# Both residual additions of a hybrid layer done by accumulating DMAs

## The chip, the cores and the metric

The kernel runs on one core of one Trainium2 chip. The metric is the device time of one execution in microseconds. Three runs of the kernel before gave 1296.79, 1296.92 and 1300.04 us; the median is 1296.92 us. TensorE is called PE, VectorE DVE, ScalarE ACT, GpSimd POOL and SyncE SP.

## The reference

One layer of a streaming encoder, for 1024 prompt tokens and 32 sample tokens (1056 columns, kept with the 1024 model channels as 8 groups of 128 partitions):

```python
xn = rmsnorm(x, pre_mix_norm_w)
proj = xn @ w_in                         # z | xBC | dt | u
# SSD heads on xBC, S5 groups on u -> y_ssd, y_s5
mix = jnp.concatenate([y_ssd, y_s5], axis=-1) @ w_out
h = x + rmsnorm(mix, post_mix_norm_w)                   # first residual addition
up, new_ffn = causal_dwconv(rmsnorm(h, pre_ffn_norm_w) @ w_up, ffn_hist, ffn_conv_w, ffn_conv_b)
gate, val = jnp.split(up, 2, axis=-1)
ffn = (jax.nn.gelu(gate, approximate=True) * val) @ w_down
y = h + rmsnorm(ffn, post_ffn_norm_w)                   # second residual addition
```

The output `y` is the tensor `yT` (128 x 8 x 1056); the states and conv histories are outputs too and are not touched by the change.

## The kernel before

Every float32 matmul is done as three matmuls on split operands (high times high, high times low, low times high): ACT makes the high part of a tile, DVE the low part. Weights come as tiles of 128x1024 (`raw`) that ACT and DVE split into `wh` and `wl` (two buffers each) or, for the down projection, `dh` and `dl`. The tokens are cut into block 0 (one chunk c0 of 512 columns) and block 1 (two chunks c1 and c2 of 272).

The stages, in the order of PE: projections and the S5 and SSD mixers (up to about 385 us); the output projection of block 0 (`gemm_outs(0)`), then its half for block 1 (`gemm_outh2`, whose 16 PSUM tiles ACT copies to `pbo`) with `post(0)` beside it; the FFN of block 0 (`ffn_block(0)`) with the second half for block 1 and `post(1)` inside it; the FFN of block 1 with the finish of block 0 (`fin0`) at its start; and the finish of block 1 (`fin1` for c1, `fin2` for c2), after which the program ends.

`post` (lines 1643 to 1675) makes `h`. For each pair j of channel groups SP loads `x` into a tile `xr` (L1655), DVE scales the branch `o` in place (L1659), POOL adds `xr` (L1660), ACT makes `xh` and DVE `xl` (L1662) for the up projection, and ACT squares `h` into `xr` (or, for the first of each sum, `pacc`), which POOL adds up (L1666) for the next norm; PE sums `pacc` over the partitions. For block 0 SP also stores `h` to the scratch tensor `hd` (L1671).

`fin_out` and `apply` (lines 1860 to 1897) make `y`. ACT has multiplied the FFN sum `acc` by the norm weight; once `sacc` (the norm's factor) is there, one engine multiplies the pair of `acc` by it (L1891) and the same engine adds `h` (L1893 from `o` for block 1, L1896 from `hr`, loaded back from `hd`, for block 0). `fp` names the pairs that POOL does: 1 and 3 of c0 and c1, 3 of c2; the others are DVE's. SP stores each pair (L1897). Three of the four pairs of c1 are held back until DVE has made the last operand of c2's norm (`issue_after`).

The order of instructions on each engine is written by a planner (`Plan`): it lists the operations that touch the same data, gives each a duration and a latency (`cost`), and schedules them forwards and backwards. The engines then run their instructions strictly in the planned order. PE's results of the stages around the change lie in four PSUM buffers (`pch2=(3, 4)`, two buffers each). The program reserves 1024 bytes of every partition as scratch for the descriptors of DMAs that POOL issues (`dynamic_dma_scratch_size=1024`, line 1937); before the change POOL issues none.

Of the kernel before, what the change touches and what calls it, by code (L numbers as in the profile page):

```python
# [9 lines left out]
F32 = mybir.dt.float32  # L10
# [8 lines left out]
KD = D_MODEL // 128  # L19
WA = 512  # L20
# [25 lines left out]
RS_A = RS_C * 2.38924456  # L46
PAR = dict(sp=('x1', 'x2', 'f2'), ia=1, d9=3, pin=1, lat=0.25, uch=1, prep0=6.809, prep1=9.9, prep2=4.066, run0=1.26, run1=6.124, run2=5.94, 
           run3=0.5, uload=6.619, swap_pool=1, z_s5=1, ssd0=13.784, ssd1=0.0, ssd2=2.778, gate0=76.032, glu0=0.384, glu1=2.807, abufs=2, 
           cvat='run7', tcat=1, late_at=2, nsq=1, fg=(), fp=((1, 3), (1, 3), (3,)), fch=(0, (0, 1), 2), pfin=0, q0=0, q1=0, q2=0, nb=0, 
           hv=(), av=(3,), post0=0.802, dn_at=((3, 0), (3, 1)), ob_at=22, sa=2, sb=1, y5b=0, cvb=2.11, msb=(1, 1, 2, 2, 2), pch0=(3,),   # L50
           pch1=(3,), pch2=(3, 4), pf=0, pb=500, pg=0, pn=500, pr=0, pairs=(1, 2, 3, 5, 6), cf=4, cb=1, cg=0, cf2=2, cb2=(0, 1), cg2=0, 
           pgt=500, p5at=1, ng=0, n12=(2, 0), cho=2, dtlag=112.5, ng2=1, pairs2=(1, 2, 3, 5, 6, 7))
# [129 lines left out]
class Plan:  # L182
# [61 lines left out]
    def read(self):  # L244
        ins = [i for i in self.tc.nc.cur_bb.bb.instructions if type(i).__name__ != "BassTilePoolBoundary"]
        n = len(ins)
        self.ins, self.pre = ins, [set() for _ in ins]
        self.eng, self.dur, self.lat = [None] * n, [0.0] * n, [0.0] * n
        self.shared, self.fset, self.bytes = [False] * n, [None] * n, [0] * n
        w, r, use = {}, {}, {}  # L250
        seen, closed = {}, {}

        def aps(l):
            out = []
            for a in l:
                if getattr(a, "bass_ap", None) is not None:
                    k = (a.bass_ap.tensor.name, a.bass_ap.offset, str(a.ap))
                    if k not in seen:
                        seen[k] = self.region(a)
                    out.append((a, seen[k]))  # L260
            return out

        for q, i in enumerate(ins):
            ia, oa = aps(i.ins), aps(i.outs)
            self.cost(q, i, ia, oa)
            for _, g in ia:
                self.pre[q].update(k for k, h in w.get(g[0], ()) if self.meet(g, h))
            for _, g in oa:
                for d in (w, r):
                    self.pre[q].update(k for k, h in d.get(g[0], ()) if self.meet(g, h))  # L270
            for _, g in oa:
                for d in (w, r):
                    d[g[0]] = [(k, h) for k, h in d.get(g[0], ()) if not self.holds(g, h)]
                w[g[0]].append((q, g))
                use.setdefault(g[0], []).append(q)
            for _, g in ia:
                r.setdefault(g[0], []).append((q, g))
                use.setdefault(g[0], []).append(q)
            if type(i).__name__ == "InstMatmult":
# [62 lines left out]
    def cost(self, q, i, ia, oa):  # L342
        self.eng[q] = e = str(i.engine).split(".")[-1]
        kind = type(i).__name__
        n = max(self.free(a) for a, _ in ia + oa)
        if kind == "InstDMACopy":
            self.bytes[q] = 4 * int(np.prod([m for _, m in ia[0][0].ap]))
            self.dur[q], self.lat[q] = 0.06, 2.0
            return
        if kind == "InstMatmult":  # L350
            n, m = (self.free(a) for a, _ in ia[:2])
            if ia[0][0].dtype == F32R:
                d = max(0.43 * n + 6, 107 if m > 64 else 54)
            elif i.is_transpose:
                d = 112
            else:
                d = 2 * max(0.85 * n, 108) if m > 64 else 0.85 * n
            self.dur[q], self.lat[q] = d * 1e-3, 0.07
            return
        big = [a for a, _ in ia if self.free(a) > 1]  # L360
        ps = any(g[0].startswith(("ms", "pm")) for _, g in ia)
        if kind == "InstActivation":
            self.fset[q] = str(i.func).split(".")[-1]
            d = 0.19 + 0.00085 * n + 0.08 * (len(ia) > len(big))
        elif e == "Pool":
            self.shared[q] = len(big) > 1
            d = 0.21 + 0.00165 * n if len(big) > 1 else 0.12 + 0.0009 * n
        else:
            self.shared[q] = not ps and n > 8
            d = 0.15 + (0.00105 if ps or len(big) > 1 else 0.00053) * n  # L370
        self.dur[q] = d

    def schedule(self, rank, pre, suc, forward=True, gate=None):
# [12 lines left out]
        while todo:  # L386
# [26 lines left out]
            start[q] = s = t  # L413
            order[e].append(q)
            if self.bytes[q]:
                if forward:
                    s = max(s, lanes[0])
                free[e] = s + self.dur[q]
                wire = max(wire, s + 0.9) + self.bytes[q] / 280e3
                end[q] = max(s + self.lat[q], wire + 0.8)  # L420
                lanes = lanes[1:] + [end[q]]
            else:
                if self.shared[q]:
                    s = max(s, lock)
# [34 lines left out]
def body(tc, xT, wt, wdt, vec, cst, dtp, hist4, hist3, h0ssd, s5p, s5bc, s5d, glu, glub,  # L459
# [286 lines left out]
    y_dram = [dram.tile([128, 4, NCH5], F32, name=f"yd{i}") for i in range(8)]  # L746
    z_dram = dram.tile([128, 4, T], F32, name="zd")
    pb_dram = dram.tile([128, KD, T - WA], F32, name="pbd")
    h_dram = dram.tile([128, KD, WA], F32, name="hd")

    ext4 = {}

# [890 lines left out]
    def post(b):  # L1643
        HN[b] = xtiles(b)
        for c in BLKC[b]:
# [6 lines left out]
            yield 2  # L1652
            for j in range(4):
                xr = iot("xr")[:, :, :w]
                D.dma_start(xr, xT[:, 2 * j:2 * j + 2, t0:t0 + w])  # L1655
                for kk in range(2):
                    k = 2 * j + kk
                    h = O[b][:, k, o:o + w]
                    V.scalar_tensor_tensor(h, h, vc("post_mix", k), r1, mult, mult)  # L1659
                    (V if k in par["hv"] else G).tensor_tensor(h, h, xr[:, kk], add)  # L1660
                    act(xh[:, k, :], h, AF.Copy, scale=vc("pre_ffn", k))
                    V.scalar_tensor_tensor(xl[:, k, :], h, vc("pre_ffn", k), xh[:, k, :].bitcast(F32), mult, sub)  # L1662
                    e = V if k in par["av"] else G
# [196 lines left out]
    def fin_out(c):  # L1860
# [13 lines left out]
        if c == 1:
            ap = [(1, j) for j in par["fp"][1]] + [(1, j) for j in range(4) if j not in par["fp"][1]][:par["ia"]]
        elif c == 2:
            ap = [(1, j) for j in range(4) if j not in par["fp"][1]][par["ia"]:] + ap
        with ExitStack() as es:
            if c == 2:
                es.enter_context(tc.issue_after(last[0].ins))  # L1880
            for c_, j in ap:
                apply(c_, j)
                yield 0.9

    def apply(c, j):
        t0, w = CHUNKS[c]
        b = int(c > 0)
        o = t0 - BLK[b][0]
        a = ACC[b][:, 2 * j:2 * j + 2, o:o + w]
        e = G if j in par["fp"][c] else V  # L1890
        e.tensor_tensor(a, a, fin[c][0][:, None, :].to_broadcast([128, 2, w]), mult)  # L1891
        if b:
            e.tensor_tensor(a, a, O[b][:, 2 * j:2 * j + 2, o:o + w], add)  # L1893
        else:
            for kk in range(2):
                e.tensor_tensor(a[:, kk], a[:, kk], hrs[2 * j + kk], add)  # L1896
        D.dma_start(yT[:, 2 * j:2 * j + 2, t0:t0 + w], a)  # L1897

    hrs = {}

    def fin_block(b):
        if b == 0:
            for j, n in enumerate(("ext0", "ext1", "W0", "G0", "T0", "C0")):
                h = tl(n, [128, 2 if j < 2 else 1, 512], "hr")
                k = 2 * j if j < 2 else j + 2
                D.dma_start(h, h_dram[:, k:k + h.shape[1]])
                for i in range(h.shape[1]):
                    hrs[k + i] = h[:, i]
# [37 lines left out]
```

## Time and profile before

| What | us |
|---|---|
| median of three runs | 1296.92 |
| the profiled execution | 1294.34 |
| its span (first to last instruction) | 1292.4 |
| PE busy | 1225.8 (95%) |
| DVE busy | 1035.2 (80%) |
| ACT busy | 574.5 (44%) |
| POOL busy | 397.7 (31%) |
| PE granted clock, mean | 0.979 |

PE is busy for 95% of the span, so the time can only change by what PE waits for, and by what lies behind PE's last matmul. The remaining 66.6 us in which PE is not busy are read stretch by stretch. A row of a timeline gives start, duration, engine, line, operation and operands; a count `x4` behind it means that four instructions are merged, and the bracket names the idle time before them and what ended it.

### The profile page before, as it was taken

The page shows a single profiled execution, that of the slowest core. Times are in us where ns is not written, and L with a number is a line of the kernel's source. Part 1 is how long each engine was busy: PE and PEld are TensorE (multiplying, and loading weights), DVE is VectorE, ACT ScalarE, POOL GpSimd, SP SyncE. Part 2 cuts the span into 40 slices and gives each one's busy share as a digit, 9 for nine tenths or more (in the row PEclk, how much of TensorE's full clock was granted, in tenths as well). Part 3 has the DMA queues.
Part 4 walks back from the last instruction along what each step waited for, and adds up shares of the span by engine and source line. Part 5 has one row for each costly group of instructions (what it writes and reads, how often), then busy time and mean ns, then how long its engine had stood idle before and what let it go on. Part 6 is the DMA issues. An engine that isn't in the chain of part 4 may idle for free.

```text
span 1292.4 us, 20981 instructions
## 1 busy us (share of the span) xinstructions
PE 1225.8 (95%) x7880; PEld 1105.6 (86%) x7880; DVE 1035.2 (80%) x1781; ACT 574.5 (44%) x979; POOL 397.7 (31%) x577
## 2 busy tenths in 40 slices
PE   6879999999998999999999999998999999999995
PEld 5768888888877888878977888887999999999994
DVE  7898887988988998987688977679577777777777
ACT  7236466554555555543444433353523333333243
POOL 5364554544146433211345110015111111111113
PEclk8989999999998999999999999999999999999997
DMA  7133323233434423234433333222323332222212
GB/s 220 57 96 99 96 76 114 79 106 93 124 105 164 152 91 99 81 104 137 153 99 123 122 99 98 95 85 82 117 81 98 99 98 82 95 86 83 82 52 70
DMA packets 66901, 132.14 MB, mean 102 GB/s; under 512 B 13936, under 2 KB 34800, under 8 KB 66800
## 3 DMA queue, kind: packets, MB, share of 16 engines
q1 hardware_dynamic: 66800, 130.81, 32.2%
q8 instruction: 62, 1.02, 0.3%
q14 instruction: 39, 0.32, 0.1%
HBM read 111.69 MB, written 15.81 MB: 99 GB/s over the span
## 4 chain that ended last, share of the span: by engine, by line
PE 79%; DVE 10%; POOL 3%; issue 3%; DMA 2%; ACT 1%; SPq 1%; DVEq 0%; ACTq 0%; POOLq 0%
PE pm L479 70%; PE ms L479 9%; DVE wl L713 1%; POOL pacc L1666 1%; POOL o L1660 1%; DVE o L1659 1%; SPq L1122 1%; DMA xst<-xT 1%; DVE scr L647 1%; DVE scr L646 1%; POOL oacc L1628 1%; PE ms L483 1%; DVE pq L996 1%; POOL hq L1164 0%; DVE yr L1104 0%
## 5 line engine op out<-in xcount | busy, mean ns | idle before, releaser
L479 PE MATMUL pm<-xh,wh 128*128 128x272 f32 (+1 forms) x1616 | 532.1, 330 | 15.9 <-ACT wh L535 8.7
L479 PE MATMUL pm<-xh,wl 128*128 128x272 f32 (+1 forms) x1616 | 531.1, 329 | 7.4 <-DVE wl L713 7.3
L479 PE MATMUL pm<-xl,wh 128*128 128x272 f32 (+1 forms) x1616 | 529.8, 328 | 1.7 <-DVE xl L1045 1.7
L479 PEld LDWEIGHTS pm<-xh,wh 128*128 128x128 f32 x1616 | 309.9, 192 | 37.8 <-ACT wh L535 8.7
L479 PEld LDWEIGHTS pm<-xh,wl 128*128 128x128 f32 x1616 | 309.0, 191 | 30.8 <-DVE wl L713 9.1
L479 PEld LDWEIGHTS pm<-xl,wh 128*128 128x128 f32 x1616 | 309.9, 192 | 24.4 <-DVE xl L1045 3.0
L535 ACT ACTIVATE wh<-raw 128x1024 fp32r<-128x1024 f32 x120 | 126.9, 1057 | 177.5 <-PE pm L479 109.5
L713 DVE TENSOR_TENSOR wl<-raw,wh 128x1024 fp32r<-128x1024 f32 x120 | 154.9, 1291 | 26.6 <-ACT wh L535 26.1
L479 PE MATMUL pm<-al,dh 128*128 128x272 f32 (+1 forms) x528 | 171.4, 325 | 0.6 <-DVE al L1751 0.6
L479 PE MATMUL pm<-ah,dh 128*128 128x272 f32 (+1 forms) x528 | 171.7, 325 | 0.3 <-ACT ah L535 0.3
L479 PE MATMUL pm<-ah,dl 128*128 128x272 f32 (+1 forms) x528 | 170.8, 324 | 0.0
L1793 DVE TENSOR_TENSOR acc<-acc,pm 128x272 f32<-128x272 f32 (+1 forms) x235 | 121.1, 520 | 53.6 <-PE pm L479 52.5
L1738 DVE SCALAR_TENSOR_TENSOR ftmp<-fext,vec_t,ftmp 128x512 f32<-128x512 f32 (+1 forms) x176 | 143.1, 814 | 3.9 <-ACT ftmp L535 2.1
L1716 POOL COPY fext<-halo 128x2 f32<-128x2 f32 x88 | 33.6, 382 | 293.0 <-DVE ftmp L1738 271.5
L1721 DVE TENSOR_TENSOR fext<-pm,rbc 128x512 f32<-128x512 f32 (+2 forms) x132 | 67.5, 511 | 69.2 <-PE pm L479 65.8
L479 PEld LDWEIGHTS pm<-ah,dh 128*128 128x128 f32 x528 | 99.4, 188 | 8.6 <-ACT ah L535 0.7
L479 PEld LDWEIGHTS pm<-al,dh 128*128 128x128 f32 x528 | 99.3, 188 | 8.1 <-DVE al L1751 0.9
L479 PEld LDWEIGHTS pm<-ah,dl 128*128 128x128 f32 x528 | 99.2, 188 | 7.7 <-issue 0.3
L535 ACT ACTIVATE dh<-raw 128x1024 fp32r<-128x1024 f32 (+1 forms) x46 | 46.7, 1018 | 108.3 <-PE pm L479 96.8
L535 ACT ACTIVATE ftmp<-fext,vec_t 128x512 f32<-128x512 f32 (+1 forms) x88 | 72.3, 822 | 11.1 <-DVE fext L1721 5.7
L535 ACT ACTIVATE ftmp<-ftmp 128x512 f32<-128x512 f32 (+1 forms) x44 | 28.4, 644 | 87.0 <-DVE ftmp L1738 87.0
L1771 DVE TENSOR_TENSOR dl<-raw,dh 128x1024 fp32r<-128x1024 f32 (+1 forms) x46 | 55.9, 1216 | 13.6 <-ACT dh L535 13.6
(318 smaller groups left out, 1668.7 us busy)
## 6 DMA issues: line engine op xcount, KB each, us to landing
raw<-wt SPq DMA_DIRECT2D x164, 512.0 KB, 3.3
gluw<-glu SPq DMA_DIRECT2D x8, 512.0 KB, 3.4
xst<-xT SPq DMA_DIRECT2D x16, 136.0 KB, 3.3
pbd<-pbo SPq DMA_DIRECT2D x8, 272.0 KB, 2.6
xr<-xT SPq DMA_DIRECT2D x8, 272.0 KB, 3.2
pbi<-pbd SPq DMA_DIRECT2D x8, 272.0 KB, 3.5
yT<-acc SPq DMA_DIRECT2D x8, 272.0 KB, 2.3
ud<-uext SPq DMA_DIRECT2D x4, 528.0 KB, 4.0
```

The costliest lines, as they stand in the source:

```text
L479: PE.matmul(out, lhsT, rhs, start=start, stop=stop, **kw)
L483: PE.transpose(out, in_, ident)
L535: S.activation(out, in_, func, bias=bias, scale=scale)
L646: e.tensor_scalar(hi[:L, o:o + L], ident[:L, :L], r[:L, i:i + 1], None, mult)
L647: last[0] = V.scalar_tensor_tensor(lo[:L, o:o + L], ident[:L, :L], r[:L, i:i + 1], hi[:L, o:o + L].bitcast(F32), mult, sub)
L713: V.tensor_tensor(lo, r, hi.bitcast(F32), sub)
L996: V.tensor_scalar(pq[lo:hi, a], src[lo:hi, :, o:o + 8], sg, None, mult)
L1716: G.tensor_copy(e[:, 0:2], halo[:, j, :])
L1721: V.tensor_tensor(e[:, 2 + o:2 + o + wp], ps[:, :wp], rbc[:, t0:t0 + wp], mult)
L1738: V.scalar_tensor_tensor(t, e[:, i:i + n], vc("fw", 3 * j + i), t, mult, add)
L1771: V.tensor_tensor(l, rr, h.bitcast(F32), sub)
L1793: V.tensor_tensor(a, a, ps[:, :w], add)
```

## The change

The scaled branch stays in `o`, and a DMA that POOL issues adds `x` to it in SBUF (`accum_op=add`): the eight scalings of a chunk go in pairs, and for each pair one DMA of 128x2x512 or 128x2x272 reads `xT` and accumulates into `o`. Nothing else reads `xT` there; `xr` is only the place for squares. The finished `h` of every chunk is stored to `yT` by SP. In the finish DVE does all the multiplications by the norm factor, and a second DMA of POOL accumulates the product onto `yT`. The additions on POOL and DVE, the scratch tensor `hd` with its loads, and the holding back of c1's pairs are gone; `fp` is empty. The planner gets a cost for POOL's DMAs (1.0 us of POOL, 3.5 us of latency), slightly other matmul costs, and an order between reads of one PSUM tile by the same engine. Since the planner works on the whole program, it writes a new order for all of it; the counts of all other instructions stay, but ACT has 21 loads of its function tables in place of 18.

```diff
-           cvat='run7', tcat=1, late_at=2, nsq=1, fg=(), fp=((1, 3), (1, 3), (3,)), fch=(0, (0, 1), 2), pfin=0, ...
+           cvat='run7', tcat=1, late_at=2, nsq=1, fg=(), fp=((), (), ()), fch=(0, (0, 1), 2), pfin=0, ...
...
             for _, g in ia:
+                if g[0].startswith(("ms", "pm")):
+                    self.pre[q].update(k for k, h in r.get(g[0], ()) if self.eng[k] == self.eng[q])
...
-            self.dur[q], self.lat[q] = 0.06, 2.0
+            self.dur[q], self.lat[q] = (0.06, 2.0) if e == "SP" else (1.0, 3.5)
...
-                d = max(0.43 * n + 6, 107 if m > 64 else 54)
+                d = max(0.426 * n + 9, 107 if m > 64 else 54)
...
-                D.dma_start(xr, xT[:, 2 * j:2 * j + 2, t0:t0 + w])
+                for kk in range(2):
+                    h = O[b][:, 2 * j + kk, o:o + w]
+                    V.scalar_tensor_tensor(h, h, vc("post_mix", 2 * j + kk), r1, mult, mult)
+                G.dma_start(O[b][:, 2 * j:2 * j + 2, o:o + w], xT[:, 2 * j:2 * j + 2, t0:t0 + w], accum_op=add)
                 for kk in range(2):
                     k = 2 * j + kk
                     h = O[b][:, k, o:o + w]
-                    V.scalar_tensor_tensor(h, h, vc("post_mix", k), r1, mult, mult)
-                    (V if k in par["hv"] else G).tensor_tensor(h, h, xr[:, kk], add)
...
-                if b == 0:
-                    D.dma_start(h_dram[:, 2 * j:2 * j + 2], O[b][:, 2 * j:2 * j + 2, o:o + w])
+                D.dma_start(yT[:, 2 * j:2 * j + 2, t0:t0 + w], O[b][:, 2 * j:2 * j + 2, o:o + w])
...
-        e = G if j in par["fp"][c] else V
-        e.tensor_tensor(a, a, fin[c][0][:, None, :].to_broadcast([128, 2, w]), mult)
-        if b:
-            e.tensor_tensor(a, a, O[b][:, 2 * j:2 * j + 2, o:o + w], add)
-        else:
-            for kk in range(2):
-                e.tensor_tensor(a[:, kk], a[:, kk], hrs[2 * j + kk], add)
-        D.dma_start(yT[:, 2 * j:2 * j + 2, t0:t0 + w], a)
+        V.tensor_tensor(a, a, fin[c][0][:, None, :].to_broadcast([128, 2, w]), mult)
+        G.dma_start(yT[:, 2 * j:2 * j + 2, t0:t0 + w], a, accum_op=add)
```

On ACT in `post(0)`, the kernel before takes each `h` soon after it is there, with copies of PE's results (`pbo`) in between:

```order
L535 ACTIVATE pbo<-pm 128x272 x2
L535 ACTIVATE pacc<-o_3883 128x512
L535 ACTIVATE xh_4057<-o_3883,vec_t 128x512
L535 ACTIVATE pbo<-pm 128x272
L535 ACTIVATE xr<-o_3883 128x512
L535 ACTIVATE xh_4057<-o_3883,vec_t 128x512
L535 ACTIVATE xr<-o_3883 128x512
L535 ACTIVATE pbo<-pm 128x272 x2
L535 ACTIVATE wh<-raw 128x1024
```

The same place of the changed kernel; the eight reads of `o` as `pacc` and `xr` are those of the four DMAs in turn, two each:

```order
L538 ACTIVATE pacc<-o_3882 128x512
L538 ACTIVATE xr<-o_3882 128x512
L538 ACTIVATE pbo<-pm 128x272 x2
L538 ACTIVATE xh_4056<-o_3882,vec_t 128x512 x2
L538 ACTIVATE xr<-o_3882 128x512
L538 ACTIVATE pacc<-o_3882 128x512
L538 ACTIVATE xr<-o_3882 128x512 x2
L538 ACTIVATE wh<-raw 128x1024
L538 ACTIVATE xr<-o_3882 128x512 x2
L538 ACTIVATE pbo<-pm 128x272 x2
```

In the changed kernel the squares of the second, third and fourth DMA, with one `wh`, stand between two groups of `pbo`.

On DVE in `post(0)`, before, the scalings (L1659) stand ahead of two splits of weights:

```order
L647 SCALAR_TENSOR_TENSOR scr<-cst_t,nry,scr 128x128
L1659 SCALAR_TENSOR_TENSOR o_3883<-o_3883,vec_t,oacc 128x512 x7
L713 TENSOR_TENSOR wl<-raw,wh 128x1024
L1659 SCALAR_TENSOR_TENSOR o_3883<-o_3883,vec_t,oacc 128x512
L713 TENSOR_TENSOR wl<-raw,wh 128x1024
```

and in the changed kernel (L716 is the split):

```order
L650 SCALAR_TENSOR_TENSOR scr<-cst_t,nry,scr 128x128
L716 TENSOR_TENSOR wl<-raw,wh 128x1024
L1659 SCALAR_TENSOR_TENSOR o_3882<-o_3882,vec_t,oacc 128x512 x8
L716 TENSOR_TENSOR wl<-raw,wh 128x1024
L1665 SCALAR_TENSOR_TENSOR xl_4057<-o_3882,vec_t,xh_4056 128x512 x2
```

One split has moved ahead of the scalings.

On POOL at the end of the program, before, after the four sums of squares (`sacc`):

```order
L1857 TENSOR_TENSOR sacc<-sacc,osq 128x272 x4
L1891 TENSOR_TENSOR acc_8887<-acc_8887,sacc 128x2x272
L1893 TENSOR_TENSOR acc_8887<-acc_8887,o_6230 128x2x272
L1891 TENSOR_TENSOR acc_8887<-acc_8887,sacc 128x2x272
L1893 TENSOR_TENSOR acc_8887<-acc_8887,o_6230 128x2x272
L1891 TENSOR_TENSOR acc_8887<-acc_8887,sacc 128x2x272
L1893 TENSOR_TENSOR acc_8887<-acc_8887,o_6230 128x2x272
```

and in the changed kernel:

```order
L1735 COPY o_4431<-fext 128x2
L1736 COPY o_4431<-fext 128x2
L1859 TENSOR_TENSOR sacc<-sacc,osq 128x272 x4
L1886 DMA yT<-acc_8850 128x2x272 x8
L1920 UNCONDITIONAL_BRANCH
```

Six tensor operations of POOL have become eight DMA issues, four of c1 and four of c2, and they are POOL's last work; on DVE the eight multiplications stand as four ahead of c2's norm and four behind it.

## Rows read from the trace of the kernel before

**Rows 1.** The page's first part: busy time, share, instructions.
```profile
span 1292.4 us, 20981 instructions
PE 1225.8 (95%) x7880; PEld 1105.6 (86%) x7880; DVE 1035.2 (80%) x1781; ACT 574.5 (44%) x979; POOL 397.7 (31%) x577
```
**Rows 2.** Busy time by stretch: PE, PEld, DVE, ACT, POOL, PE clock, DMA share, GB/s.
```profile
0.00:385.00 385.00, 349.30 (x2245) 309.93 (x2246) 327.76 (x576) 202.45 (x420) 177.39 (x208) 0.97 0.36 106
385.00:440.00 55.00, 48.97 (x322) 45.10 (x321) 46.77 (x62) 27.22 (x48) 36.59 (x21) 0.94 0.46 154
640.00:715.00 75.00, 71.43 (x369) 58.27 (x368) 62.12 (x130) 33.15 (x63) 38.12 (x43) 1.00 0.39 121
870.00:925.00 55.00, 49.55 (x361) 47.96 (x361) 44.95 (x69) 23.88 (x38) 25.13 (x30) 0.94 0.31 106
1255.00:1292.40 37.40, 21.51 (x168) 20.35 (x166) 27.46 (x61) 14.24 (x34) 12.79 (x10) 0.76 0.18 60
```
**Rows 3.** PE's longest waits at 385 to 445 and 875 to 925: total, times, longest.
```profile
PE pm L479 <- DVE wl L713: 4.2, 1, 4.2
...
PE pm L479 <- DVE fext L1721: 4.1, 1, 4.1
```
**Rows 4.** Timeline in post(0): start, us, engine, line, operation, idle before.
```profile
399.70 0.40 ACT L535 ACTIVATE pbo<-pm 128x272 f32<-128x272 f32 x1 [1.11 <-PE pm L479]
401.77 9.92 DVE L1659 SCALAR_TENSOR_TENSOR o<-o,vec_t,oacc 128x512 f32<-128x512 f32 x7 [1.22 <-ACT oacc L535]
411.61 2.28 DVE L713 TENSOR_TENSOR wl<-raw,wh 128x1024 fp32r<-128x1024 f32 x1
420.62 3.97 POOL L1660 TENSOR_TENSOR o<-o,xr 128x512 f32<-128x512 f32 x2
```
**Rows 5.** DMA issues with KB each and us to landing; one stretch of SP.
```profile
xr<-xT SPq DMA_DIRECT2D x8, 272.0 KB, 3.2
xr<-xT SPq DMA_DIRECT2D x4, 512.0 KB, 3.6
yT<-acc SPq DMA_DIRECT2D x8, 272.0 KB, 2.3
xst<-xT SPq DMA_DIRECT2D x8, 256.0 KB, 5.1
...
2.12 6.30 SPq L1041 DMA_DIRECT2D xst<-xT  x11
```
**Rows 6.** Timeline of post(1): scalings and last sums of both chunks; PE's first wait.
```profile
655.28 2.77 DVE L1659 SCALAR_TENSOR_TENSOR o<-o,vec_t,oacc 128x272 f32<-128x272 f32 x4
666.36 4.10 POOL L1666 TENSOR_TENSOR pacc<-pacc,xr 128x272 f32<-128x272 f32 x3
670.52 1.23 PE L479 MATMUL ms<-onec,pacc 128*128 128x1 f32 x12 [0.98 <-POOL pacc L1666]
682.74 2.76 DVE L1659 SCALAR_TENSOR_TENSOR o<-o,vec_t,oacc 128x272 f32<-128x272 f32 x4
698.89 2.59 POOL L1666 TENSOR_TENSOR pacc<-pacc,xr 128x272 f32<-128x272 f32 x2
```
**Rows 7.** Timeline of DVE in fin0.
```profile
889.36 1.22 DVE L1891 TENSOR_TENSOR acc<-acc,sacc 128x1024 f32<-128x1024 f32 x1
890.62 4.49 DVE L1896 TENSOR_TENSOR acc<-acc,hr 128x512 f32<-128x512 f32 x2
```
**Rows 8.** Timeline of the finish of block 1.
```profile
1273.55 1.58 DVE L1891 TENSOR_TENSOR acc<-acc,sacc 128x544 f32<-128x544 f32 x1
1276.35 13.36 SPq L1897 DMA_DIRECT2D yT<-acc  x8
1282.46 0.40 ACT L535 ACTIVATE sacc<-ms 128x272 f32<-128x272 f32 x1 [7.76 <-PE ms L479]
1287.84 0.72 DVE L1891 TENSOR_TENSOR acc<-acc,sacc 128x544 f32<-128x544 f32 x1
```
**Rows 9.** The group of ACT's table loads: busy, mean ns.
```profile
L535 ACT ACT_TABLE_LOAD x18 | 23.1, 1283 | 10.6 <-DVE yr L900 6.1 <-DMA xst<-xT 4.2
```

More of the change, by code (lines that the diff above doesn't have):

```diff
@@ L48 @@
            run3=0.5, uload=6.619, swap_pool=1, z_s5=1, ssd0=13.784, ssd1=0.0, ssd2=2.778, gate0=76.032, glu0=0.384, glu1=2.807, abufs=2,
-           cvat='run7', tcat=1, late_at=2, nsq=1, fg=(), fp=((1, 3), (1, 3), (3,)), fch=(0, (0, 1), 2), pfin=0, q0=0, q1=0, q2=0, nb=0,
+           cvat='run7', tcat=1, late_at=2, nsq=1, fg=(), fp=((), (), ()), fch=(0, (0, 1), 2), pfin=0, q0=0, q1=0, q2=0, nb=0,
            hv=(), av=(3,), post0=0.802, dn_at=((3, 0), (3, 1)), ob_at=22, sa=2, sb=1, y5b=0, cvb=2.11, msb=(1, 1, 2, 2, 2), pch0=(3,),
@@ L415, in schedule @@
             if self.bytes[q]:
-                if forward:
+                if forward and e == "SP":
                     s = max(s, lanes[0])
@@ L419, in schedule @@
                 wire = max(wire, s + 0.9) + self.bytes[q] / 280e3
-                end[q] = max(s + self.lat[q], wire + 0.8)
-                lanes = lanes[1:] + [end[q]]
+                end[q] = max(s + self.dur[q] + self.lat[q], wire + 0.8)
+                if e == "SP":
+                    lanes = lanes[1:] + [end[q]]
             else:
@@ L748, in body @@
     pb_dram = dram.tile([128, KD, T - WA], F32, name="pbd")
-    h_dram = dram.tile([128, KD, WA], F32, name="hd")
     ext4 = {}
@@ L1873, in fin_out @@
         ap = [(c, j) for j in range(4)]
[L1874 to L1883, printed above, removed]
+        for c_, j in ap:
+            apply(c_, j)
+            yield 0.9
     def apply(c, j):
@@ L1889, in apply @@
         a = ACC[b][:, 2 * j:2 * j + 2, o:o + w]
-        e = G if j in par["fp"][c] else V
-        e.tensor_tensor(a, a, fin[c][0][:, None, :].to_broadcast([128, 2, w]), mult)
-        if b:
-            e.tensor_tensor(a, a, O[b][:, 2 * j:2 * j + 2, o:o + w], add)
-        else:
-            for kk in range(2):
-                e.tensor_tensor(a[:, kk], a[:, kk], hrs[2 * j + kk], add)
-        D.dma_start(yT[:, 2 * j:2 * j + 2, t0:t0 + w], a)
-    hrs = {}
-    def fin_block(b):
[L1902 to L1908, printed above, removed]
+        V.tensor_tensor(a, a, fin[c][0][:, None, :].to_broadcast([128, 2, w]), mult)
+        G.dma_start(yT[:, 2 * j:2 * j + 2, t0:t0 + w], a, accum_op=add)
+    def fin_block(b):
         for c in BLKC[b]:
```

## The prediction

> **What bounds the kernel now.** I read the page's first part, then the busy time by stretch, then in each stretch with idle time what PE waited for, and last the timelines there. PE is busy for 1225.8 of 1292.4 us [rows 1], so 66.6 us are all that a change can win from PE's waits and the tail. Five stretches hold them: 35.7 up to 385 us, 6.0 around `post(0)`, 3.6 around `post(1)`, 5.5 around `fin0` and 15.9 in the last 37.4 (length less PE's busy time) [rows 2]. The change acts in the last four. In `post(0)` the largest wait of PE is 4.2 us for a `wl`, in `fin0` 4.1 us for a `fext` [rows 3]. The `wl` starts at 411.61 and stands directly behind seven scalings that took 9.92 [rows 4]. DVE's row in `fin0` shows the like: 1.22 and 4.49 us of finish work in one piece [rows 7]. In `post(1)` PE waits 0.98 for the last sum of squares [rows 6]. At the end PE has nothing left: the order is factor, products, additions and stores, and the last store's issue ends at 1289.71 (1276.35 + 13.36) [rows 8], 2.7 before the span's end.
>
> **The open price: how fast POOL can issue accumulating DMAs.** No row shows POOL issuing any DMA, nor any accumulating one; all terms of the sum but one hang on the time from one such DMA to the next, which I call p. SP's loads of the same 272 KB land 3.2 us after issue, 512 KB 3.6; a store of 272 KB lands after 2.3 [rows 5]. SP hands over eleven loads in 6.30, 0.57 each, while each takes 5.1 to land [rows 5]: SP waits for no landing. For POOL I assume that it does: the program leaves 1024 bytes of a partition for descriptors, and each of these DMAs names 256 rows as source and, to add, the same rows of the destination as a second source. So p is an issue and a landing: 0.57 + 3.2 = 3.8 us, for 512 KB 4.2, by the rows that are nearest. Bounds: 2.3, if the landing is that of a store and the issue lies inside it; 6.9, if the issue takes as long as a sum on POOL (4.10 / 3 = 1.37 [rows 6]) and destination's read and write follow each other (1.37 + 3.2 + 2.3); for 512 KB 7.3.
>
> No row shows such a limit. [...]
>
> **The tail, +12.7.** Before, DVE could take the first product of c1 at 1273.55 [rows 8]. Its rows of 128x544 take 0.72 where POOL does not work beside (1.58 where it does) [rows 8]; in the changed kernel POOL makes no sums there, so the first DMA can be issued at 1274.27. POOL has eight, four of c1, four of c2. At one per 3.8 the last lands at 1274.27 + 30.4 = 1304.7; c2's products cannot be late, since its factor is there at 1282.86 (1282.46 + 0.40) [rows 8], and POOL's fifth DMA starts at 1289.5. Of the 2.7 behind the last issue before, 2.3 were landing [rows 5], so 0.4 stay: 1305.1, against 1292.4. What went, additions of 0.72 to 1.87, was itself shorter than a DMA. Bounds: p = 2.3 gives 1293.1 (+0.7), p = 6.9 gives 1329.9 (+37.5).
>
> **`post(0)`, +2.4.** The `wl` has moved ahead of the scalings, and these no longer have POOL's sums beside them (9.92 / 7 = 1.42 each; 0.72 by the row of a similar size [rows 4, 8]): the wait of 4.2 goes. What is late next is ACT, which copies PE's results out (`pbo`). From 401.77 the first pair is scaled at 403.2; its DMA lands at 407.4 and two squares (0.40 each by ACT's row [rows 4]) end at 408.2. Then come two `pbo`, and the next stand behind the squares of the other three DMAs, which land 4.2 apart: 408.2 + 12.6 = 420.8. PE has four buffers, each 1.5 us of its work (0.40 + 1.11, ACT's rhythm there [rows 4]), so 6.0 of 12.6 are covered and 6.6 are a new wait. Net +2.4. The chain itself is no later: the last DMA lands at 403.2 + 16.8 = 420.0, and before, POOL's last sum ended at 424.59 [rows 4]. Bounds: with all of it hidden -4.2; with 7.3 for a DMA 21.9 - 6.0 - 4.2 = +11.7. SP's store of `h` replaces that to `hd`, at nothing: SP is not what anything waits for.
>
> **`post(1)`, +6.0.** Four scalings take 2.77 and 2.76 [rows 6], so the first pair of c1 is there at 656.7, of c2 at 684.1. Four DMAs later (15.2) two squares (0.8) and two sums (2.59 [rows 6]) follow: 675.3 and 702.7. Before, the sums ended at 670.46 and 701.48 [rows 6], the first already 0.98 too late for PE. So +4.8 and +1.2, the second on top since all behind the first shifts. ACT's splits and gelu and POOL's `halo` copies queue behind the same DMAs; I cost them at nothing, as the FFN's next tiles cover them, and they become a cost if that cover goes. Bounds: -1.0 (the wait goes) and, at p = 6.9, 17.2 + 13.6 = +30.8.
>
> **`fin0`, -4.1.** DVE has four products of 1.22 and none of the additions (4.49 for two [rows 7]); POOL issues between its small copies. The wait for `fext` goes. Bounds: -4.1 and 0, if `fext`'s copies on POOL stand behind DMAs for as long.
>
> **The rest, 0.** Up to 385 us the work is re-planned with three more table loads of 1.283 us [rows 9], 3.8 us if all were on PE's path; the waits there (35.7) can move by as much the other way: 0, bounds of 4 to either side.
>
> Sum: 12.7 + 2.4 + 6.0 - 4.1 = +17.0. The profiled execution took 1294.34 (span and 1.94), so 1311.3. It lay 2.6 under the median of 1296.92, so I forecast 1313.9. Each us of p is worth 19 (8 in the tail, 3, and 4 twice).
>
> **Rivals.** *POOL hands over as SP does*, 0.57 apart. For it: that SP's rows show it, and that nothing in the trace shows a limit for POOL. Then the `wl` wait goes (-4.2), `post(1)` loses its 0.98, `fin0` 4.1, and at the end c2's factor at 1282.86 is followed by four products of 0.72, one issue, one landing of 3.2 and the 0.4: 1289.9, -2.5. Together -11.8: 1285.1, faster. It decides as soon as two DMAs are in flight at once.
>
> *One at a time, but short*: p = 2.9 (0.57 and a store's 2.3). Tail 1274.27 + 23.2 + 0.4, +5.5; `post(0)` 9.9 (3.3 each) - 10.2 = -0.3; `post(1)` +1.2; `fin0` -4.1; sum +2.3, 1299.2. Against it: loads of these sizes needed 3.2 and 3.6. [...]
>
> *Long*: the accumulate reads, then writes, and POOL's issue is as slow as its sums. From p = 5.0 on: 1313.9 + 1.2 x 19 = 1337, up to 1381 with all upper bounds.
>
> *The new order decides*: waits up to 385 us change by 4, with p as in the second rival, 1295 to 1303.
>
> **How the numbers follow.** A measurement of this kernel can tell 0.3%, 3.9 us, from no change: 1293.0 to 1300.8. Chances: the forecast 0.55 (p from 3.0 to 5.0, 1299 to 1337), POOL back to back 0.18, short 0.14, long 0.08, the order 0.05. Faster is the first rival and the lowest part of the short one, 0.22; the same, most of the short one and part of the order, 0.11; slower 0.67. The range goes from the first rival's 1285 to 1338, and leaves out the long case and what lies below.
>
> **What would show it.** In the tail: eight issues of L1886 some 3.8 us apart, each at the landing of the one before, the chain of waits ending in POOL's last DMA, and DVE idle. Issues 1 us apart or less prove the first rival. In `post(0)`: ACT waiting for `o` from a DMA, PE for `pbo`; in `post(1)` PE waiting 5 us or more for `pacc`. The waits of 4.2 for `wl` and 4.1 for `fext` should be gone; if either stands, that term is wrong. If the last issue of POOL lies before 1287, the sum is wrong as a whole.

## The result and the profile after

The changed kernel takes 1349.74 us (median of 4 runs, 1346.77 to 1351.18) against 1298.48 of the kernel before, run beside it: a ratio of 1.039, interval 1.0361 to 1.0419. It is slower, as forecast, but by three times as much: the forecast was +17.0 us, its range ended at 1338, and the profiled execution is 56.8 us longer by span (1349.2 against 1292.4).

The page's first part of the changed kernel, in the columns of [rows 1]:

```profile
span 1349.2 us, 20951 instructions
PE 1234.8 (92%) x7880; PEld 1113.5 (83%) x7880; DVE 1008.1 (75%) x1777; ACT 575.4 (43%) x982; POOL 364.1 (27%) x565
```

DVE and POOL have less to do than before (27.1 and 33.6 us less) and the kernel is longer: their busy time is not what counts. PE is now idle for 114.4 us (66.6 before), which is 47.8 of the 56.8 us; the other 9.0 are longer busy time of the same 7880 matmuls, at a mean granted clock of 0.955 (0.979 before). By stretch, in the columns of [rows 2]:

```profile
0.00:385.00 385.00, 348.75 (x2216) 308.77 (x2217) 329.28 (x571) 200.41 (x418) 169.00 (x204) 0.96 0.35 101
385.00:440.00 55.00, 35.65 (x242) 33.01 (x240) 27.27 (x41) 18.39 (x34) 25.77 (x17) 0.86 0.57 143
640.00:715.00 75.00, 66.90 (x390) 58.65 (x390) 48.16 (x116) 30.91 (x58) 23.81 (x31) 0.93 0.45 122
```

In the first stretch PE is idle for as long as it was (36.3 us, 35.7 before), but does 29 matmuls fewer there; `post(0)` has 19.4 us of idle PE where it had 6.0, and the granted clock of that stretch fell from 0.94 to 0.86. The third holds the first half of `post(1)`'s waits (8.1 idle, 3.6 before). PE's longest waits (total, times, longest), where before there was 4.2 for `wl` and 4.1 for `fext` [rows 3]:

```profile
PE pm L482 <- ACT pbo L538: 19.1, 1, 19.1
PE ms L482 <- POOL pacc L1669: 17.2, 2, 9.1
...
PE pm L482 <- ACT acc L538: 2.2, 2, 2.0
...
PE pm L482 <- DVE wl L716: 1.2, 1, 1.2
```

The waits that were to go are gone (`wl` 1.2 in all, `fext` 0.3), and two others add up to 36.3 us: `pbo`, which is new, and `pacc`, which was 2.3 before. The timeline of `post(0)` in the changed kernel shows DVE's scalings, POOL's issues and what ACT waits for (start, duration, engine, line; the bracket is the idle time before it and what ended it):

```profile
406.77 5.39 DVE L1659 SCALAR_TENSOR_TENSOR o<-o,vec_t,oacc 128x512 f32<-128x512 f32 x8
```

```profile
408.51 1.41 POOL L1660 DMA_DIRECT2D o<-xT  x1 [7.87 <-DVE o L1659]
415.80 1.23 POOL L1660 DMA_DIRECT2D o<-xT  x1 [5.88 <-issue]
425.11 1.21 POOL L1660 DMA_DIRECT2D o<-xT  x1 [8.07 <-issue]
432.06 1.22 POOL L1660 DMA_DIRECT2D o<-xT  x1 [5.74 <-issue]
```

```profile
416.68 0.67 ACT L538 ACTIVATE pbo<-pm 128x272 f32<-128x272 f32 x2
417.23 1.33 ACT L538 ACTIVATE xh<-o,vec_t 128x512 fp32r<-128x512 f32 x2
424.93 0.63 ACT L538 ACTIVATE xr<-o 128x512 f32<-128x512 f32 x1 [6.36 <-DMA o<-xT]
425.46 0.61 ACT L538 ACTIVATE pacc<-o 128x512 f32<-128x512 f32 x1
431.82 1.15 ACT L538 ACTIVATE xr<-o 128x512 f32<-128x512 f32 x2 [5.74 <-DMA o<-xT]
432.87 1.04 ACT L538 ACTIVATE wh<-raw 128x1024 fp32r<-128x1024 f32 x1
438.84 1.15 ACT L538 ACTIVATE xr<-o 128x512 f32<-128x512 f32 x2 [4.93 <-DMA o<-xT]
439.90 0.66 ACT L538 ACTIVATE pbo<-pm 128x272 f32<-128x272 f32 x2
```

DVE had scaled all eight groups by 412.2 (406.77 + 5.39), yet POOL issues its fourth DMA at 432.06: the DMAs come 7.3, 9.3 and 7.0 us apart, each "issue" of the bracket being a wait for nothing that the profile shows. ACT has no `pbo` between 417.3 and 439.9, so PE's four buffers stay full and PE waits 19.1 us. The tail has the same picture; the first product and six of the eight issues are

```profile
1307.33 0.72 DVE L1885 TENSOR_TENSOR acc<-acc,sacc 128x544 f32<-128x544 f32 x1
```

```profile
1308.46 1.21 POOL L1886 DMA_DIRECT2D yT<-acc  x1 [3.31 <-DVE sacc L1859]
1313.31 1.22 POOL L1886 DMA_DIRECT2D yT<-acc  x1 [3.63 <-DVE nry L629]
1318.15 1.21 POOL L1886 DMA_DIRECT2D yT<-acc  x1 [3.62 <-DVE acc L1885]
...
1333.00 1.22 POOL L1886 DMA_DIRECT2D yT<-acc  x1 [3.81 <-issue]
1338.01 1.21 POOL L1886 DMA_DIRECT2D yT<-acc  x1 [3.79 <-issue]
1342.94 1.22 POOL L1886 DMA_DIRECT2D yT<-acc  x1 [3.72 <-issue]
```

They are 4.8 to 5.0 us apart, 4.93 on average, while DVE has finished the last product at 1318.1. (The first waits for its product. The releasers named in the next two brackets only happen to end just before: c1's four products were there at 1310.3, and neither `nry` nor c2's products are read by these DMAs. The even spacing suggests that from the second on all wait for the same thing.) The DMA table has the landing times, counted from the start of the issue, to be set beside [rows 5]:

```profile
o<-xT POOLq DMA_DIRECT2D x8, 272.0 KB, 4.7
yT<-o SPq DMA_DIRECT2D x8, 272.0 KB, 2.4
yT<-acc POOLq DMA_DIRECT2D x8, 272.0 KB, 4.6
...
o<-xT POOLq DMA_DIRECT2D x4, 512.0 KB, 6.9
yT<-o SPq DMA_DIRECT2D x4, 512.0 KB, 3.0
yT<-acc POOLq DMA_DIRECT2D x4, 512.0 KB, 6.0
```

In the tail the next issue starts 0.3 us after the landing of the one before. So the mechanism of the forecast stands (one accumulating DMA at a time) and its price does not: 4.93 in place of 3.8, and 7.0 to 9.3 in place of 4.2.

### The profile page after: what moved, and what is told of

Same layout as the page of the kernel before. It is cut to its first block, busy times and chain, and to the rows that moved or that the text cites. A ratio compares the mean times of both kernels' runs of the same rounds, so it can differ in the third digit from the quotient of the medians.

```text
span 1349.2 us, 20951 instructions
## 1 busy us (share of the span) xinstructions
PE 1234.8 (92%) x7880; PEld 1113.5 (83%) x7880; DVE 1008.1 (75%) x1777; ACT 575.4 (43%) x982; POOL 364.1 (27%) x565
## 4 chain that ended last, share of the span: by engine, by line
PE 72%; DVE 10%; issue 7%; DMA 4%; ACT 3%; POOL 2%; SPq 1%; POOLq 0%; ACTq 0%; DVEq 0%
PE pm L482 62%; PE ms L482 9%; DMA o<-xT 2%; SPq L1124 1%; DVE wl L716 1%; DMA raw<-wt 1%; ACT wh L538 1%; POOL yT L1886 1%; DVE R L1164 1%; PE ms L486 1%; DVE xl L1047 0%; DVE scr L649 0%; DMA yT<-acc 0%; DVE ftmp L1740 0%; ACT xh L538 0%
## 5 line engine op out<-in xcount | busy, mean ns | idle before, releaser
L482 PE MATMUL pm<-xh,wh 128*128 128x272 f32 (+1 forms) x1616 | 532.5, 330 | 28.8 <-ACT pbo L538 19.1
L482 PEld LDWEIGHTS pm<-xh,wh 128*128 128x128 f32 x1616 | 310.5, 192 | 51.5 <-ACT pbo L538 19.3
L716 DVE TENSOR_TENSOR wl<-raw,wh 128x1024 fp32r<-128x1024 f32 x120 | 156.1, 1301 | 48.4 <-ACT wh L538 48.2
L1740 DVE SCALAR_TENSOR_TENSOR ftmp<-fext,vec_t,ftmp 128x512 f32<-128x512 f32 (+1 forms) x176 | 138.4, 787 | 13.9 <-ACT ftmp L538 11.6
```

What stands on the lines that cost most here:

```text
L482: PE.matmul(out, lhsT, rhs, start=start, stop=stop, **kw)
L716: V.tensor_tensor(lo, r, hi.bitcast(F32), sub)
L1740: V.scalar_tensor_tensor(t, e[:, i:i + n], vc("fw", 3 * j + i), t, mult, add)
```

## The experiments

Theory A: POOL's descriptor room holds one accumulating DMA of 256 rows, so each waits for the landing of the one before. Rival B: POOL waits for a landing whatever the room. Beside it stands the question how much of the loss is the new order of the whole program. The edits of the first four runs, against the changed kernel (e1) or as the part of the change that is kept (e2 to e4, main lines only):

```diff
 e1
-    nc = bacc.Bacc("TRN2", target_bir_lowering=False, num_devices=1, dynamic_dma_scratch_size=1024)
+    nc = bacc.Bacc("TRN2", target_bir_lowering=False, num_devices=1, dynamic_dma_scratch_size=1536)
 e2: the kernel before with
+                if g[0].startswith(("ms", "pm")):
+                    self.pre[q].update(k for k, h in r.get(g[0], ()) if self.eng[k] == self.eng[q])
...
-                d = max(0.43 * n + 6, 107 if m > 64 else 54)
+                d = max(0.426 * n + 9, 107 if m > 64 else 54)
...
-                end[q] = max(s + self.lat[q], wire + 0.8)
+                end[q] = max(s + self.dur[q] + self.lat[q], wire + 0.8)
...
 e3: e2 with
...
+                G.dma_start(O[b][:, 2 * j:2 * j + 2, o:o + w], xT[:, 2 * j:2 * j + 2, t0:t0 + w], accum_op=add)
...
 e4: e2 with
...
+        G.dma_start(yT[:, 2 * j:2 * j + 2, t0:t0 + w], a, accum_op=add)
...
```

The third edit of e2 belongs to the planner's cost of DMAs: it also lets SP's DMAs end up to 0.06 us later in the plan.

**e1, more room.** 

> The changed kernel with 1536 instead of 1024 bytes of descriptor room, nothing else (the planned order is the same). Theory A (room for one accumulating DMA only, so POOL's next one waits for the landing, 4.96 us apart in the tail): two fit, the spacing in the tail falls to about 2.5 us, the tail shortens by some 17 us, the waits of PE for pbo (19.1) and pacc (17.2) fall by about half, in all about 1300 to 1315 us. Rival B (POOL waits for a landing whatever the room): spacing stays at 4.9 and the time at 1345 to 1352 us.

Measured: 1305.18 us, 1.0066 (1.004 to 1.0092) of before. The order of the instructions is that of the changed kernel; 512 bytes take 44.6 us away. POOL in the tail:

```profile
1284.10 2.46 POOL L1886 DMA_DIRECT2D yT<-acc  x2 [3.31 <-DVE sacc L1859]
1288.97 1.21 POOL L1886 DMA_DIRECT2D yT<-acc  x1 [2.41 <-DVE nry L629]
1291.28 1.20 POOL L1886 DMA_DIRECT2D yT<-acc  x1 [1.09 <-issue]
1293.92 1.22 POOL L1886 DMA_DIRECT2D yT<-acc  x1 [1.44 <-DVE acc L1885]
```

Two issues stand back to back, the third follows 4.9 us after the first, when that has landed: two in flight, 2.4 us apart on average. PE's wait for `pbo` is 10.2 and for `pacc` 4.8. Theory A as expected, B is out.

**e2, the plan alone.** 

> The kernel before with only the planner's changed costs and the order between reads of a PSUM tile; no accumulating DMA. Theory A (the first scaling of post(0) came 5.0 us later in the changed kernel because the new order is worse up to there): 1300 to 1304 us. Rival (the new order is neutral and the 5 us come from something that the DMAs bring): 1294 to 1299 us.

Measured: 1306.64 us, 1.0067 (1.0047 to 1.0087): a loss of 9.9 without any DMA of POOL, above the range of 1300 to 1304 that I expected. Its first scaling starts at 412.9 (401.8 before), and ACT has 26 loads of its function tables (18 before).

**e3, the first addition alone.** 

> Planner as changed, the first addition by accumulating DMAs, the finish as in the kernel before. Theory A: the PE waits for pbo and pacc stand (some 30 us more than before), the tail is as before, 1325 to 1338 us. Rival (the loss sits in the finish and in the tail alone): under 1310 us.

Measured: 1334.9 us, 1.0286 (1.0248 to 1.0324), 28.3 over e2. PE's two waits are there as in the changed kernel, 18.6 for `pbo` and 18.3 for `pacc`, and `fext`'s of 4.0 stays, as DVE keeps its additions in `fin0`.

**e4, the second addition alone.** 

> Planner as changed, post as in the kernel before (with h stored to yT), the second addition by accumulating DMAs. Theory A: the tail costs some 23 us, fin0's wait for fext goes (-4), 1313 to 1325 us. Rival (the tail is late only because the stages ahead delay it): 1295 to 1303 us.

Measured: 1325.96 us, 1.0222 (1.0188 to 1.0257), just over the expected range; 19.3 over e2. Its eight DMAs in the tail start at 1284.45 to 1318.95, 4.93 apart. The parts add up: 1306.6 + 28.3 + 19.3 = 1354.2, against 1349.7 for both.

**e5, DMAs of half the rows, 1024 bytes.** In the changed kernel, each DMA is cut by channel group:

```diff
-                G.dma_start(O[b][:, 2 * j:2 * j + 2, o:o + w], xT[:, 2 * j:2 * j + 2, t0:t0 + w], accum_op=add)
+                    G.dma_start(h, xT[:, 2 * j + kk, t0:t0 + w], accum_op=add)
...
-        G.dma_start(yT[:, 2 * j:2 * j + 2, t0:t0 + w], a, accum_op=add)
+        for kk in range(2):
+            G.dma_start(yT[:, 2 * j + kk, t0:t0 + w], a[:, kk], accum_op=add)
```

> The changed kernel with 1024 bytes of room as it is, each accumulating DMA of 256 rows cut into two of 128 rows (24 + 24 in place of 12 + 12). Theory A (POOL waits because the room is full; the run with 1536 bytes took 2 DMAs of 256 rows, so 1024 bytes should take three or so of 128 rows): first three issues back to back at 1.2 us, then pairs of halves some 2.5 to 3.5 us apart in place of 4.96, 1308 to 1325 us. Rival B (one DMA at a time, whatever its size; more room only helped in another way): each half about 4 us, a pair 8 us, the tail 20 us longer than in the changed kernel, over 1370 us.

Measured: 1320.11 us, 1.0181 (1.0131 to 1.0231): twice as many DMAs and 29.6 us less than the changed kernel. POOL in the tail:

```profile
1295.10 2.70 POOL L1887 DMA_DIRECT2D yT<-acc  x3
1298.67 0.86 POOL L1887 DMA_DIRECT2D yT<-acc  x1 [0.87 <-issue]
```

Three go out without a gap, and the fourth starts 3.57 us after the first, whose kind lands after 3.5. So it is the room that counts. A half has half the bytes too, but in `post(0)` of this run the halves have 256 KB each, nearly the 272 KB of which only one is in flight in the changed kernel, and again three go out:

```profile
414.98 2.88 POOL L1660 DMA_DIRECT2D o<-xT  x3 [7.09 <-DVE o L1659]
421.16 0.89 POOL L1660 DMA_DIRECT2D o<-xT  x1 [3.30 <-issue]
```

So the room is used by rows and not by bytes: three halves are in flight here, one DMA of 256 rows in the changed kernel, two in e1. My estimate from these counts, if nothing but the room holds POOL and equal DMAs take equal shares of it: one of 256 rows takes over 512 and at most 768 of the bytes reserved in a partition, one of 128 rows over 256 and at most 341.

**e6, the plan told the truth, 1024 bytes.**

```diff
-            self.dur[q], self.lat[q] = (0.06, 2.0) if e == "SP" else (1.0, 3.5)
+            self.dur[q], self.lat[q] = (0.06, 2.0) if e == "SP" else (5.0, 0.1)
```

> The changed kernel with 1024 bytes of room, but the planner is told what the trace of the changed kernel showed: POOL is taken for 5.0 us by an accumulating DMA and the data is there 0.1 us later (1.0 and 3.5 before). Theory A (ACT's order is planned for DMAs that overlap, so that pbo and pacc stand behind data that come later): the waits of 19.1 and 17.2 fall by a third or more, the tail stays, 1325 to 1342 us. Rival (the chains themselves set the time, no order can hide them): 1345 to 1352 us.

Measured: 1325.84 us, 1.0222 (1.0184 to 1.0261). PE's wait for `pbo` fell from 19.1 to 6.3, that for `pacc` is gone, and the tail's issues are 4.9 apart as before. So 23.9 of the 51 us go when the plan takes POOL's DMAs one at a time. The new order differs elsewhere too (the first scaling comes at 409.7, 2.9 later than in the changed kernel, and PE waits 6.1 for `acc`), so the share that lies in planning for DMAs that overlap is not exact.

**e7 and e8, which edit of the planner costs.** e7 is the kernel before with the order rule of e2 alone; e8 is e1 with the matmul cost of before.

> The kernel before with only the order between reads of a PSUM tile by one engine in the planner; matmul costs as before, no accumulating DMA. If that order rule is what costs 9.9 us in the planner-only run: 1303 to 1310 us; if the matmul cost (0.426 n + 9) is: 1294 to 1300 us.

> The changed kernel with 1536 bytes of room and the matmul cost of before (0.43 n + 6); all else as changed. If the matmul cost is what the planner-only run lost 9.9 us by, 1293 to 1298 us; if it is the order rule, or the loss is no property of one edit but of any new order, 1301 to 1310 us.

Measured: e7 1300.19 us, 1.0018 (0.9992 to 1.0044), not to be told from no change and 0.2 above the second answer's range; e8 1313.83 us, 1.0124 (1.0084 to 1.0164). By e2 and e7 the matmul cost (with the 0.06 us of SP's DMAs) loses 6 us, by e8 and e1 the same cost gains 9: neither of e8's answers came. What a new order costs is no property of one edit, nor does it lie in one place: e8's first scaling is no later than e1's (406.0, 407.1), but its wait for `pacc` is 11.4 (4.8). The first scaling lay between 401.2 and 414.8 in the runs.

**e9, plain copies.** The changed kernel without `accum_op=add`.

> The changed kernel with 1024 bytes of room, POOL's 24 DMAs as plain copies in the same places of the same order (both residual additions are left out: o and yT are overwritten). Theory A (an accumulate fills the room twice, by source and by destination as second source): plain copies go three at a time as the halves did, spacing in the tail under 2.5 us, landing some 2.3 to 3.2 us for 272 KB in place of 4.7, 1303 to 1315 us. Rival (the room goes by rows, adding or not): still one at a time, spacing 2.5 to 4.5 by the shorter landing, 1318 to 1345 us.

Measured: 1285.01 us, 0.9912 (0.9897 to 0.9927), 18 us below the range of A. Its first issues in the tail, and the landing times:

```profile
1268.70 0.72 POOL L1886 DMA_DIRECT2D yT<-acc  x1 [3.30 <-DVE sacc L1859]
1269.69 1.46 POOL L1886 DMA_DIRECT2D yT<-acc  x2 [0.27 <-issue]
1271.65 0.72 POOL L1886 DMA_DIRECT2D yT<-acc  x1 [0.51 <-issue]
```

```profile
o<-xT POOLq DMA_DIRECT2D x8, 272.0 KB, 3.7
yT<-acc POOLq DMA_DIRECT2D x8, 272.0 KB, 2.8
o<-xT POOLq DMA_DIRECT2D x4, 512.0 KB, 7.2
yT<-acc POOLq DMA_DIRECT2D x4, 512.0 KB, 4.3
```

Three in flight in the same 1024 bytes, so the same rows take less room when nothing is added; the issue takes 0.72 in place of 1.21 and the landing on `yT` 2.8 in place of 4.6. The accumulate thus costs three times: in room, at issue and, onto `yT`, at landing. For 512 KB onto `o` the landing is no shorter (7.2 with up to three in flight, 6.9 for the accumulating ones alone). The order is that of the changed kernel, instruction for instruction, and the first scaling comes as late (407.5); behind it nothing is lost once the DMAs are cheap. But the additions are not done here, so 1285 is no time that this kernel can have.

**e10 and e14, block 0's second addition alone.** The kernel before with e7's rule and the planner's cost of DMAs; `h` of block 0 goes to `yT`, `hd` and its loads are gone, and DVE does all products of c0; block 1 is finished as before. e10 has 1536 bytes, e14 1024.

```diff
...
         if b:
             e.tensor_tensor(a, a, O[b][:, 2 * j:2 * j + 2, o:o + w], add)
+            D.dma_start(yT[:, 2 * j:2 * j + 2, t0:t0 + w], a)
         else:
-            for kk in range(2):
-                e.tensor_tensor(a[:, kk], a[:, kk], hrs[2 * j + kk], add)
-        D.dma_start(yT[:, 2 * j:2 * j + 2, t0:t0 + w], a)
+            G.dma_start(yT[:, 2 * j:2 * j + 2, t0:t0 + w], a, accum_op=add)
```

> The kernel before with only block 0's second addition by accumulating DMAs (h of block 0 stored to yT, no hd, no hr loads; 1536 bytes; matmul cost of before, order rule between PSUM reads). Theory A (nothing on PE's path waits for these four DMAs, DVE loses 4.5 us of additions per pair of c0): the wait of 3 to 4 us for fext goes and nothing comes in its place, 3 to 5 us under the order-only run of 1300.2 (1295 to 1298). Rival (the halo copies queued behind POOL's DMAs hold fext as long): 1299 to 1304 us.

> The run with only block 0's second addition by accumulating DMAs, with the room as it was, 1024 bytes. Theory A (its four DMAs stand apart, between fext copies, so that one at a time is enough, or nearly): 1294 to 1299 us, clearly not slower than before. Rival (the second to fourth DMA hold POOL's halo copies for 6 us each, and those hold fext): 1300 to 1310 us.

Measured: e10 1295.35 us, 0.998 (0.9956 to 1.0003); e14 1297.43 us, 0.9997 (0.9979 to 1.0015). Both are far faster than the changed kernel; neither is clearly faster than the one before. In e10 PE waits for nothing between 870 and 940 (e7: 3.3 for `fext`), in e14 1.9 for `acc`. e14's four DMAs stand 6.2 to 6.7 us apart (898.41, 905.15, 911.45, 917.62) and nothing on PE's path needs them: one at a time is cheap there.

**e11, a latency by bytes, 1536 bytes.**

```diff
-            self.dur[q], self.lat[q] = (0.06, 2.0) if e == "SP" else (1.0, 3.5)
+            self.dur[q], self.lat[q] = (0.06, 2.0) if e == "SP" else (1.2, 1.1 + self.bytes[q] / 116e3)
```

> The changed kernel with 1536 bytes and the planner's POOL DMA cost set to what the traces show (1.2 us of POOL, then 1.1 us and 1 us per 116 KB: 3.5 for 272 KB, 5.6 for 512 KB). Theory A (of the 10.2 us that PE still waited for pbo in the 1536-byte run, the wrong latency in the plan is the cause): that wait falls under 4 us, 1296 to 1302 us. Rival (two in flight are too few, the order cannot help): 1303 to 1308 us.

Measured: 1311.7 us, 1.0122 (1.0093 to 1.0152): the wait for `pbo` fell from 10.2 to 5.7 only, other waits came with the new order (`ge` 6.6), and the whole is slower than e1. It fits neither answer.

**e12, e11 with block 1 finished as before.**

> As the run before, but block 1 is finished as in the kernel before (additions on DVE and POOL, stores by SP); the first addition and that of block 0 by accumulating DMAs. Theory A (in the tail eight DMAs at 2.4 us are still later than sums and stores): the end after c1's factor falls back from 21 to some 20 us, 1 to 5 us under the run before, 1293 to 1300 us. Rival (with two in flight the tail is no later than before): the same as the run before within 2 us.

Measured: 1308.02 us, 1.0091 (1.0076 to 1.0106), 3.7 under e11: within A's 1 to 5, but the two intervals overlap, so this does not decide between A and the rival. The time in all is outside A's range because e11 had missed.

**e13, halves and 1536 bytes.**

> The changed kernel with halves of 128 rows and 1536 bytes: five of them in flight by the theory (three with 1024). Theory A (the spacing is then set by the issue, 0.9 us for a half): halves about 0.9 to 1.0 us apart in the tail in place of 1.27, PE's wait for pbo under 4 us, 1298 to 1310 us, at least 10 us under the run with halves and 1024 bytes. Rival (three in flight are enough, the DMA engines are the limit): spacing as before, 1315 to 1322 us.

Measured: 1305.17 us, 1.0056 (1.0034 to 1.0079), 14.9 under e5. POOL's tail, its start in `post(0)`, and PE's wait for `pbo`:

```profile
1282.41 7.18 POOL L1887 DMA_DIRECT2D yT<-acc  x8
1290.92 7.15 POOL L1887 DMA_DIRECT2D yT<-acc  x8 [1.33 <-DVE acc L1885]
```

```profile
413.18 4.66 POOL L1660 DMA_DIRECT2D o<-xT  x5 [7.08 <-DVE o L1659]
419.26 0.89 POOL L1660 DMA_DIRECT2D o<-xT  x1 [1.42 <-issue]
```

```profile
PE pm L482 <- ACT pbo L538: 4.7, 2, 3.0
```

Eight halves in 7.18 us, 0.90 each with no gap: in the tail the room no longer limits, and what is late there is the products of c2. In `post(0)`, where landings are longer (9.2 for 256 KB), five go out without a gap and the sixth waits, until 0.23 us after ACT has taken up the first one's data (419.03): five in flight, as expected (the estimate under e5 leaves four or five). `pbo` missed "under 4" by 0.7. The kernel is still 7 us over the one before. Its first scaling comes at 412.1, 10.3 later than before, and its profiled span is 10.7 longer (1303.1 against 1292.4), so the loss lies ahead of the first accumulating DMA.

## Why the prediction was wrong

The way was right and the mechanism too; the size was not. The step that failed is the price of one accumulating DMA: "So p is an issue and a landing: 0.57 + 3.2 = 3.8 us, for 512 KB 4.2, by the rows that are nearest." The rows show an issue of 1.22 and a landing, counted from the issue's start, of 4.6; the next follows 0.3 later, 4.93 in all. For 512 KB in `post(0)` it is 7.0 to 9.3. The nearest rows were those of plain DMAs of SP, and e9 shows how little they say: a plain copy to `yT` from POOL lands in 2.8 us where the accumulating one needs 4.6. My upper bound for 272 KB (6.9) held; that for 512 KB (7.3) did not: in `post(0)` one spacing was 9.3. That only one such DMA fits into 1024 bytes was an assumption of mine: no row of before shows it, and no run shows that the destination's rows fill the room as a second source. What the runs show is one of 256 rows in flight in 1024 bytes (the issues 4.93 us apart), two in 1536 (e1), and three plain ones of the same rows in 1024 (e9).

By my own "each us of p is worth 19", p = 4.93 makes 17.0 + 21.5 = 38.5, some 1335 us, still inside the range. What carried the time out of it are two other terms: the 512 KB DMAs of `post(0)` with a cover that was too large, 9.1 more than that rule gives, and "The rest, 0", which was 5.0, outside its bounds of 4.

**The tail.** Forecast +12.7. From DVE's first product to the end it was 18.9 before (1273.55 to 1292.4) and is 41.9 (1307.33 to 1349.2): +23.0. Put 4.93 into my working and it gives 12.7 + 8 x 1.13 = 21.7. That POOL starts where the first product ends (0.4 later) and that c2's products are never late for it was right.

**`post(0)`.** Forecast +2.4; it is 19.1 of waiting in place of 4.2, +14.9. The chain was as written (two `pbo` after the first pair's squares, the next behind the fourth DMA's), with 22.6 us between the two groups (417.3 to 439.9) where I had 12.6; and of my 6.0 us of cover 3.5 were there. The `wl` wait went, as said, and eight scalings without POOL's sums beside them took 5.39 where seven had taken 9.92. The last DMA landed about 14 us after the time at which POOL's last sum had ended before, against my 4.6 us ahead of it: "the chain itself is no later" fell too.

**`post(1)`.** Forecast +6.0; PE waits 17.2 for `pacc`, 2.3 before, +14.9. With the spacing of 5.0 measured there my working gives 6.0 + 2 x 4 x 1.2 = 15.6.

**`fin0`.** Forecast -4.1, and the wait for `fext` of 4.1 is gone; 2.2 of waiting for `acc` is new.

**The rest.** Forecast 0; the first scaling comes 5.0 later (401.77 to 406.77), 406.8 to 407.5 in all runs of this order (e1 and e9 too), and no DMA of POOL comes before it, so it is the order and not the DMAs. I had costed the new order by its table loads. Their number ahead of 400 us goes along with the time of the first scaling in all 16 traces, though not strictly: 7 loads 401.2 to 401.8, 8 loads 406.8 to 408.2, 9 loads 405.0 to 406.4, 11 loads 409.7, 13 loads 410.8 to 412.8, 15 loads 412.1 to 414.8. One load more (8 for 7 here) is 1.28 us and cannot by itself be 5.0; no run changes the loads alone.

Sum: 23.0 + 14.9 + 14.9 - 4.1 + 2.2 + 5.0 = 55.9 of 56.8. Landmarks that both traces have give the whole: the changed kernel is late by 5.0 at the first scaling, by 20.6 at that of `post(1)` (655.28 to 675.85), by 37.4 at PE's second sum over `pacc` (701.54 to 738.95), by 33.8 at the first product of the tail, and by 56.8 at the end. The steps are 5.0, 15.6, 16.8, -3.6 and 23.0. The two of `post` hold more than their waits, and PE is slow behind these: in `post(1)` its granted clock was 0.50 from 699.4 to 704.4 and from 739 to 745, behind waits of 8.1 and 9.2, and 1.00 from 704.4 to 720.

Of the rivals, POOL handing over as SP does is excluded at 1024 bytes by the changed kernel's own rows, and at 1536 it holds for two DMAs (e1). By its time the long case, which I gave 0.08, is what happened; by p for 272 KB the run lies just inside the forecast's own band of 3.0 to 5.0, and by p for 512 KB above it. The long case names a reason (the accumulate reads, then writes); e9 shows that a landing on `yT` is 1.8 shorter without the accumulate, but no run shows which part of it takes the time. I took the row that looked alike for the row that is near. In hindsight the middle of the two bounds, (2.3 + 6.9) / 2 = 4.6, would have been a better choice than the end that other engines' DMAs suggested.

Not settled: whether the table loads are what moves the stages ahead of 400 us by up to 13 us from order to order; why a 512 KB DMA onto `o` needs 7.0 to 9.3 (plain copies, up to three in flight, took 7.2 in e9 as well); and whether a room for three or more DMAs of 256 rows would do better than halves, which was not tried.

## What to carry to other kernels

In no run here that does the additions did accumulating DMAs make the kernel clearly faster. An accumulating DMA on GpSimd is not a free addition: count how many fit into the descriptor room that the program reserves, and if it is one, each costs its whole landing on the queue (4.93 us from one of 272 KB to the next in the changed kernel's tail), and a plan that believes they overlap puts other engines' work behind them (PE's wait for `pbo` was 19.1 us with such a plan, 6.3 in e6). A little more room (512 bytes of a partition: 44.6 us here) or fewer rows per DMA (29.6 us) were worth far more here than the engine time that the DMAs saved. Use it where nothing waits for the result and the DMAs stand apart (block 0's finish here), not in a chain and not at the end of the program.

## What the runs showed of the hardware

- Issue on POOL: 1.21 us for an accumulating DMA of 256 rows, 0.72 for a plain one (e9), 0.88 for an accumulating one of 128 rows (e5). Landing of 272 KB on `yT`: 4.6 accumulating, 2.8 plain; of 136 KB 3.5 accumulating (e5).
- In 1024 bytes of room one accumulating DMA of 256 rows is in flight (the changed kernel, issues 4.93 us apart), or three of 128 rows (of 136 or 256 KB alike, e5), or three plain ones of 256 rows (e9); in 1536 bytes two of 256 rows (e1) or five of 128 rows (e13).
- While POOL waits for room the profile shows an idle engine (3.4 to 8.1 us before an issue in the changed kernel), its wait put down to "issue" or to a releaser whose data the DMA does not read; a regular spacing near the landing time (4.93 us against 4.6 in the changed kernel's tail) gives it away.
- More of them in flight can land later: 512 KB onto `o` took 6.9 us one at a time and 9.9 with two in flight (e1), 136 KB onto `yT` 3.5 with three and 4.6 with up to five in flight (e5, e13). 272 KB onto `yT` took 4.6 either way.
